# Exposed attention: one key tile of ten keeps its softmax weights whole, and its product with the values runs in fp32

## Chip, cores, metric

One core of one Trainium2 chip runs the kernel. The time is the device time of one execution in microseconds (us); the kernel before took 2972.27 us, the median of 3 runs (2970.56 to 2973.72).

## What is computed

A two-layer trunk over 1024 latent tokens and 256 context tokens, width 1024. Layer 0 mixes tokens with a convolution module, layer 1 with grouped-query attention (16 query heads of 64, 4 key/value heads); each layer ends in a SwiGLU FFN. The change touches the attention of layer 1 only:

```python
def gqa_sdpa(q, k, v):
    B, Q, H, Dh = q.shape
    qg = q.reshape(B, Q, N_KV_HEADS, KV_GROUP, Dh)
    s = jnp.einsum("bqkgd,bskd->bkgqs", qg, k).astype(jnp.float32) * (Dh ** -0.5)
    p = jax.nn.softmax(s, axis=-1).astype(v.dtype)
    o = jnp.einsum("bkgqs,bskd->bqkgd", p, v)
    return o.reshape(B, Q, H * Dh)
```

All 1280 keys (1024 latent, 256 context) take part for each latent query. Everything is fp32 in the reference.

## The kernel before

Matmuls run mostly in the type fp32r, which keeps fewer mantissa bits. So each operand is split into a high part (rounded to fp32r) and a low part (what is left), and a product is made of high x high, high x low and low x high. For softmax weights times values the kernel does less: the value tile holds high parts in its first 64 columns and low parts in the other 64 (`self.vst`, tile HR), so one matmul with the high part of the weights (L996) and one with the low part (L997) give all the products; the two halves are added at the end (L1007, L1008).

The attention works in **units**: one key/value head `t` (4) and one block of 128 queries `q` (8), with the 4 query heads of that group; 32 units in all. A first stream takes 16 units (blocks 0 to 3), a second one the other 16. A unit has two halves:

- `scores` (L959 to L983), for each of its 4 heads: q times k into 1280 columns of PSUM, as three chunks of 512, 512 and 256 columns with two matmuls each (L972); then VectorE scales, writes the row to SBUF and takes its minimum (L978), and ScalarE makes the exponential (L980).
- `values` (L985 to L1014), for each of ten key tiles `j` of 128 keys: four 128x128 transposes into one PSUM bank (L990), a ScalarE copy that rounds to the high part (L993), a VectorE subtraction that makes the low part (L994), and the two matmuls into the accumulator (L996, L997). After the tenth: the sums' reciprocal (L1001), a GpSimd copy that spreads it (L1003), two ScalarE copies and two VectorE additions that join the halves (L1007, L1008), two transposes (L1011), the final scaling (L1012) and the transfer to DRAM (L1279).

The generator `attn_stream` interleaves the `scores` of one unit with the `values` of the unit before. A list scheduler then sets the order on each engine by priority; the two value matmuls are pushed back by `self.lav` = 40 places. The first stream starts beside the rest of the q/k/v projections (`qr`, the background queue). When that queue is empty the stage is **exposed**: nothing but attention runs, and PSUM (8 banks of 512 fp32 columns) is shared out so: two score slots at columns 0 to 1279 and 1280 to 2559 (`sring = [0, TOK]`), which meet in bank 2 (columns 1024 to 1535), banks 5 and 6 for transposes, bank 7 for the accumulator. High and low parts go round in four slots (`ptring`, tile T2). The `values` of 15 of the first 16 units run in this exposed stage, from about 1655 to 1870 us. The second stream runs beside the output projection and the FFN and is not touched.

Short names below: **S512** and **S256** are score matmuls of 512 and 256 columns, **T** is one transpose, **AV** one value matmul. The S256 chunk of each slot lies in bank 2, which it shares with the other slot; it waits for the L978 that reads the other slot.

Of the kernel before, what the change touches and what calls it, by code (L numbers as in the profile page):

```python
# [8 lines left out]
F32 = mybir.dt.float32  # L9
# [45 lines left out]
class Kern:  # L55
# [928 lines left out]
    def values(self, t, Ps, sums, dst, done):  # L984
        nc, c = self.nc, self.c  # L985
        av = self.bank("av")
        for j in range(NJ):
            tp = self.bank("pt")
            for h in range(4):
                nc.tensor.transpose(tp[:, h * P:(h + 1) * P], Ps[h][:, j * P:(j + 1) * P], c["ident"])  # L990
            ph, pl = self.ptring[self.ptslot % len(self.ptring)]
            self.ptslot += 1
            nc.scalar.copy(ph, tp)  # L993
            nc.vector.tensor_tensor(pl, tp, ph.bitcast(F32), op=ALU.subtract)  # L994
            with self.later(self.lav):
                nc.tensor.matmul(av, lhsT=self.vst[:, t, j, :], rhs=ph, start=j == 0, stop=False)  # L996
                nc.tensor.matmul(av, lhsT=self.vst[:, t, j, :], rhs=pl, start=False, stop=j == NJ - 1)  # L997
            yield 0.87

        r = sums[:, 1, :]  # L1000
        nc.vector.reciprocal(r, sums[:, 0, :])  # L1001
        rx = self.sb(256)
        nc.gpsimd.tensor_copy(rx.rearrange("p (h d) -> p h d", d=HD), r.unsqueeze(2).to_broadcast([P, 4, HD]))  # L1003
        tmp = self.sb(256).rearrange("p (a q) -> p a q", q=P)
        v = av.rearrange("p (a b q) -> p a b q", b=2, q=P)
        for b, r, o in ((0, slice(0, 64), slice(64, 128)), (1, slice(64, 128), slice(0, 64))):
            nc.scalar.copy(tmp[r], v[o, :, b, :])  # L1007
            nc.vector.tensor_tensor(dst[r], v[r, :, b, :], tmp[r], op=ALU.add)  # L1008
        rb = self.bank("av")
        for a in range(2):  # L1010
            nc.tensor.transpose(rb[:, a * P:(a + 1) * P], rx[:, a * P:(a + 1) * P], c["ident"])  # L1011
        nc.vector.tensor_tensor(dst, dst, rb[:, 0:256].rearrange("p (a q) -> p a q", q=P), op=ALU.mult)  # L1012
        done()
        yield 0.1  # L1014
# [244 lines left out]
    def attention(self, final, qr):  # L1259
        nc, a, c = self.nc, self.a, self.c  # L1260
# [11 lines left out]
        def dst(q0):  # L1272
            def of(t, q):
                if (t, q % 4) == (NKV - 1, 3):
                    return self.olast, lambda: None
                st = self.sb(256).rearrange("p (a q) -> p a q", q=P)

                def done():
                    nc.gpsimd.dma_start(self.od[:, 2 * t:2 * t + 2, q * P:(q + 1) * P], st)  # L1279
                return st, done  # L1280
            return of
# [5 lines left out]
        self.sring = [TOK]  # L1287
        self.pring = [pr1[:, 0], prh[:, 0], pr1[:, 1], prh[:, 1], pr1[:, 2], prh[:, 2], prh[:, 3]]
        self.rate = 0.8
        self.lav = 40  # L1290
        self.bgq.append(qr)
        pr4 = None
        for us in self.attn_stream(units, (self.kub, kbuf), dst(0), True):
            if self.bgq:
                self.pump(self.rate * us)
            elif pr4 is None:
                pr4 = self.T("T5", [P, 3, TOK])
                self.pring = self.pring[:4] + [pr4[:, 0], pr4[:, 1], pr4[:, 2]] + self.pring[4:]
                self.set_banks(**alone)
                self.sring = [0, TOK]  # L1300
        self.lav = 40

        self.lo_dve = 1.0
        self.set_banks(mm=[6], st=[6], pt=[5], av=[7])
# [168 lines left out]
```

## Time and profile before

| what | value |
|---|---|
| median of 3 runs | 2972.27 us (2970.56 to 2973.72) |
| profiled execution, its own time | 2968.5 us |
| its span | 2966.6 us |
| TensorE (PE) busy | 2883.0 us, 97% |
| VectorE (DVE) busy | 1928.0 us, 65% |
| ScalarE (ACT) busy | 1197.4 us, 40% |
| GpSimd (POOL) busy | 240.6 us, 8% |
| exposed attention, two units | 29.40 us |

The profiled execution lies 3.8 us below the median of the three runs. The shares are means over the whole span. Matmul durations in the trace overlap, since matmuls are pipelined and their ends are modelled: what a matmul costs PE is the distance from its start to the next start. A transpose that follows another kind, or is followed by one, has its neighbour's start recorded some 0.1 us early.

### The profile page before, as it was taken

The numbers are of one execution on the slowest core, as the hardware profiler recorded it, in microseconds if no ns is written. First come the engines' busy times: TensorE is split into PE (matmuls) and PEld (weight loads), VectorE is DVE, ScalarE is ACT, GpSimd is POOL, SyncE is SP. The second block draws the span as 40 slices with busy tenths as digits, with TensorE's granted clock in tenths as the row PEclk, the third lists the DMA queues.
The fourth block names the chain that finished last, engine by engine and source line by source line (L and its number), as shares of the span: only waits on it lengthen the run. The fifth ranks groups of instructions, "written<-read, shape, count | busy, mean of one in ns | idle before, by whom it ended". The sixth has DMA issues, their size and how long they took to land.

```text
span 2966.6 us, 38934 instructions
## 1 busy us (share of the span) xinstructions
PE 2883.0 (97%) x14914; PEld 2399.0 (81%) x14914; DVE 1928.0 (65%) x3397; ACT 1197.4 (40%) x1966; POOL 240.6 (8%) x387
## 2 busy tenths in 40 slices
PE   8999989999999999999999999989999999999997
PEld 6888877888888888888877777767777778888886
DVE  6887887857555367333587899786666657543335
ACT  5222265532222135222344788645555543332222
POOL 0000001011112010000013111100100000000000
PEclk9999999999999999999999999989999999999999
DMA  6443434334355234333444211322212143442332
GB/s 246 134 123 97 122 129 168 116 115 136 127 167 174 65 124 156 97 96 96 134 163 161 61 49 45 107 79 79 84 56 84 62 136 108 146 142 93 95 97 64
DMA packets 132138, 336.35 MB, mean 113 GB/s; under 512 B 31472, under 2 KB 53008, under 8 KB 130800
## 3 DMA queue, kind: packets, MB, share of 16 engines
q1 hardware_dynamic: 78624, 222.59, 23.4%
q0 software_dynamic: 29408, 103.83, 10.7%
q10 hardware_dynamic: 23920, 7.44, 1.1%
q8 instruction: 117, 1.92, 0.3%
q14 instruction: 69, 0.57, 0.1%
HBM read 289.50 MB, written 38.93 MB: 111 GB/s over the span
## 4 chain that ended last, share of the span: by engine, by line
PE 87%; DVE 7%; issue 3%; DMA 1%; ACT 1%; POOL 0%; ACTq 0%; SPq 0%; DVEq 0%; POOLq 0%
PE ps L170 20%; PE ps L171 20%; PE ps L172 20%; PE ps L972 4%; PE ps L990 4%; PE ps L996 2%; PE ps L997 2%; PE ps L440 2%; PE ps L441 2%; PE ps L442 2%; PE ps L518 1%; PE ps L651 1%; PE ps L181 1%; PE ps L182 1%; PE ps L183 1%
## 5 line engine op out<-in xcount | busy, mean ns | idle before, releaser
L172 PE MATMUL ps<-T,wl 128*128 128x512 f32 (+1 forms) x2032 | 764.4, 376 | 4.8 <-DVE wl L146 4.8
L170 PE MATMUL ps<-T,wh 128*128 128x512 f32 (+1 forms) x2032 | 767.1, 378 | 0.5 <-DVE sm L794 0.4
L171 PE MATMUL ps<-T,wh 128*128 128x512 f32 (+1 forms) x1984 | 745.4, 376 | 0.0
L142 ACT CAST wh<-wr 128x1024 fp32r<-128x1024 f32 x285 | 299.3, 1050 | 747.5 <-PE ps L171 549.0
L146 DVE TENSOR_TENSOR wl<-wr,wh 128x1024 fp32r<-128x1024 f32 x279 | 341.2, 1223 | 284.3 <-ACT wh L142 279.5
L172 PEld LDWEIGHTS ps<-T,wl 128*128 128x128 f32 x2032 | 384.1, 189 | 74.8 <-DVE wl L146 5.2
L170 PEld LDWEIGHTS ps<-T,wh 128*128 128x128 f32 x2032 | 384.3, 189 | 69.7 <-ACT T L1333 1.7
L171 PEld LDWEIGHTS ps<-T,wh 128*128 128x128 f32 x1984 | 375.1, 189 | 67.2 <-DVE T L162 1.3
L171 PE MATMUL ps<-HS,wh 128*128 128x512 f32 (+1 forms) x768 | 297.4, 387 | 0.0
L994 DVE TENSOR_TENSOR T<-ps,T 128x512 fp32r<-128x512 f32 x320 | 216.9, 687 | 112.0 <-ACT T L993 111.2
L170 PE MATMUL ps<-HS,wh 128*128 128x512 f32 (+1 forms) x720 | 277.8, 388 | 0.0
L172 PE MATMUL ps<-HS,wl 128*128 128x512 f32 (+1 forms) x720 | 277.8, 386 | 0.0
L993 ACT CAST T<-ps 128x512 fp32r<-128x512 f32 x320 | 186.0, 586 | 195.0 <-PE ps L990 181.6
L990 PE MATMUL ps<-cst,T 128*128 128x128 f32 x1100 | 190.3, 275 | 4.6 <-DVE T L994 4.6
L978 DVE TENSOR_SCALAR_CACHE_REDUCE T<-ps,rq 128x1280 f32<-128x1280 f32 x110 | 170.0, 1546 | 27.4 <-PE ps L972 21.7
L825 DVE TENSOR_TENSOR T<-ps,T 128x512 f32<-128x512 f32 (+1 forms) x168 | 110.4, 663 | 115.5 <-PE ps L172 115.0
L990 PEld LDWEIGHTS ps<-cst,T 128*128 128x128 f32 x1100 | 133.4, 141 | 51.5 <-DVE T L994 32.5
L800 DVE TENSOR_TENSOR sm<-sm,ps 128x256 f32<-128x256 f32 (+1 forms) x88 | 54.6, 620 | 181.3 <-PE ps L172 181.2
L980 ACT ACTIVATE T<-T,mn 128x1280 f32<-128x1280 f32 x110 | 150.3, 1366 | 40.8 <-DVE T L978 40.3
L171 PEld LDWEIGHTS ps<-HS,wh 128*128 128x128 f32 x768 | 144.5, 188 | 27.4 <-DVE HS L162 0.2
L172 PEld LDWEIGHTS ps<-HS,wl 128*128 128x128 f32 x720 | 135.3, 188 | 26.8
L170 PEld LDWEIGHTS ps<-HS,wh 128*128 128x128 f32 x720 | 135.0, 188 | 26.1 <-ACT HS L159 0.8
(274 smaller groups left out, 4672.6 us busy)
## 6 DMA issues: line engine op xcount, KB each, us to landing
wr<-in_w SPq DMA_DIRECT2D x220, 512.0 KB, 3.5
q<-in_w SPq DMA_DIRECT2D x44, 512.0 KB, 3.4
wr<-in_pw SPq DMA_DIRECT2D x35, 512.0 KB, 3.6
HR<-in_wmodT POOLq DMA_DIRECT2D x56, 256.0 KB, 3.8
q<-in_wmodT POOLq DMA_DIRECT2D x56, 256.0 KB, 3.9
q<-qsd POOLq DMA_DIRECT2D x32, 256.0 KB, 3.2
wr<-in_wo SPq DMA_DIRECT2D x16, 512.0 KB, 3.4
qsd<-T POOLq DMA_DIRECT2D x14, 512.0 KB, 3.7
```

The lines of the kernel that those rows point to most:

```text
L142: nc.scalar.copy(hi, raw)
L146: nc.vector.tensor_tensor(lo, raw, hi.bitcast(F32), op=ALU.subtract)
L170: nc.tensor.matmul(out[:, :n], lhsT=wh, rhs=xh, start=k == 0, stop=False)
L171: nc.tensor.matmul(out[:, :n], lhsT=wh, rhs=xl, start=False, stop=False)
L172: nc.tensor.matmul(out[:, :n], lhsT=wl, rhs=xh, start=False, stop=k == nk - 1)
L825: nc.vector.tensor_tensor(yd, out[:, :c1 - c0], yd, op=ALU.add)
L972: nc.tensor.matmul(sc[:, k0:k0 + w], lhsT=q[:, h, :], rhs=kt[:, p * TOK + k0:p * TOK + k0 + w], start=p == 0, stop=p == 1)
L978: nc.vector.tensor_scalar(out=pt, in0=sc, scalar1=rq[:, h:h + 1], scalar2=None, op0=ALU.mult, op1=ALU.min, accum_out=mn)
L980: nc.scalar.activation(pt, pt, AF.Exp, bias=mn, scale=-1.0, accum_out=sums[:, 0, h:h + 1])
L990: nc.tensor.transpose(tp[:, h * P:(h + 1) * P], Ps[h][:, j * P:(j + 1) * P], c["ident"])
L993: nc.scalar.copy(ph, tp)
L994: nc.vector.tensor_tensor(pl, tp, ph.bitcast(F32), op=ALU.subtract)
```

## The change

In the exposed stage `self.whole` is `(5,)`, elsewhere it is empty. For key tile `j = 5` of each unit in that stage, the transposed weights are copied by ScalarE to a scratch tile `sm` in fp32, not rounded; the VectorE subtraction is left out; and one fp32 matmul, with the value tile read as fp32, takes the place of the two fp32r ones. The amount that the generator yields for this tile is 1.28, not 0.87; it would pace background work, and in this stage there is none.

```diff
@@ values
                 nc.tensor.transpose(tp[:, h * P:(h + 1) * P], Ps[h][:, j * P:(j + 1) * P], c["ident"])
+            if j in self.whole:
+                w = self.sm(512)
+                nc.scalar.copy(w, tp)
+                with self.later(self.lav):
+                    nc.tensor.matmul(av, lhsT=self.vst[:, t, j, :].bitcast(F32), rhs=w, start=False, stop=False)
+                yield 1.28
+                continue
             ph, pl = self.ptring[self.ptslot % len(self.ptring)]
@@ attention
         self.rate = 0.8
+        self.whole = ()
         self.lav = 40
@@ attention, where the background queue is empty
                 self.sring = [0, TOK]
+                self.whole = (5,)
         self.lav = 40
+        self.whole = ()
```

In the changed program the new matmul is L995 and stands 15 times; the lines after it are 7 higher (L994 becomes L1001, L996 and L997 become L1003 and L1004, L1001 becomes L1008, L1008 becomes L1015, L1011 becomes L1018, L1012 becomes L1019). The scheduler also orders the stage anew.

VectorE, around the end of one unit of the exposed stage. `T_12403` is the ring of high and low parts, `T_12401` and `T_12900` are weight buffers, `sb` the unit's result. Before:

```order
L978 TENSOR_SCALAR T_12401,mn<-ps,rq_9315 128x1280
L994 TENSOR_TENSOR T_12403<-ps,T_12403 128x512
L1008 TENSOR_TENSOR sb<-ps,sb 64x256
L994 TENSOR_TENSOR T_12403<-ps,T_12403 128x512
L978 TENSOR_SCALAR T_12900,mn<-ps,rq_9315 128x1280
L1008 TENSOR_TENSOR sb<-ps,sb 64x256
L994 TENSOR_TENSOR T_12403<-ps,T_12403 128x512
L1012 TENSOR_TENSOR sb<-sb,ps 128x256
L994 TENSOR_TENSOR T_12403<-ps,T_12403 128x512
L978 TENSOR_SCALAR T_12900,mn<-ps,rq_9315 128x1280
```

and with the change, at the same place:

```order
L978 TENSOR_SCALAR T_12401,mn<-ps,rq_9315 128x1280
L1001 TENSOR_TENSOR T_12403<-ps,T_12403 128x512 x2
L1015 TENSOR_TENSOR sb<-ps,sb 64x256
L1008 RECIPROCAL sums<-sums 128x4
L978 TENSOR_SCALAR T_12900,mn<-ps,rq_9315 128x1280
L1015 TENSOR_TENSOR sb<-ps,sb 64x256
L1001 TENSOR_TENSOR T_12403<-ps,T_12403 128x512
L1019 TENSOR_TENSOR sb<-sb,ps 128x256
L1001 TENSOR_TENSOR T_12403<-ps,T_12403 128x512
L978 TENSOR_SCALAR T_12900,mn<-ps,rq_9315 128x1280
```

The reciprocal has moved ahead of the L978 in the middle; two subtractions and one addition still stand before that L978.

TensorE, at the same place: from one slot's score matmuls to the transposes that end the unit. Before:

```order
L972 MATMUL ps<-T_12400,q 128x512 x4
L972 MATMUL ps<-T_12400,q 128x256 x2
L972 MATMUL ps<-T_12400,q 128x512 x2
L990 MATMUL ps<-cst,T_12401 128x128
L990 MATMUL ps<-cst,T_12900 128x128 x3
L972 MATMUL ps<-T_12400,q 128x512 x2
L990 MATMUL ps<-cst,T_12401 128x128
L990 MATMUL ps<-cst,T_12900 128x128 x3
L972 MATMUL ps<-T_12400,q 128x256 x2
L972 MATMUL ps<-T_12400,q 128x512
L1011 MATMUL ps<-cst,sb 128x128 x2
```

and with the change:

```order
L972 MATMUL ps<-KB,q 128x256 x2
L972 MATMUL ps<-KB,q 128x512 x2
L990 MATMUL ps<-cst,T_12401 128x128
L990 MATMUL ps<-cst,T_12900 128x128 x3
L972 MATMUL ps<-KB,q 128x512 x2
L990 MATMUL ps<-cst,T_12401 128x128
L990 MATMUL ps<-cst,T_12900 128x128 x3
L972 MATMUL ps<-KB,q 128x512 x4
L972 MATMUL ps<-KB,q 128x256 x2
L972 MATMUL ps<-KB,q 128x512
L1018 MATMUL ps<-cst,sb 128x128 x2
```

Before, the last S256 pair belongs to slot 1, and between the end of slot 0's six matmuls and it stand S512 x2, four T, S512 x2 and four T. With the change it belongs to slot 0, and between the last S512 of slot 1 and it stand four T and S512 x4.

## Rows read from the trace of the kernel before

**Rows 1.** The page: span, busy time of PE and DVE, and the shares of the chain that ended last by engine.

```profile
span 2966.6 us, 38934 instructions
...
PE 2883.0 (97%) x14914; PEld 2399.0 (81%) x14914; DVE 1928.0 (65%) x3397; ACT 1197.4 (40%) x1966; POOL 240.6 (8%) x387
...
PE 87%; DVE 7%; issue 3%; DMA 1%; ACT 1%; POOL 0%; ACTq 0%; SPq 0%; DVEq 0%; POOLq 0%
```

**Rows 2.** Busy time of each engine in stretches of two units of the exposed stage: stretch and its length, PE, PEld (weight loads), DVE, ACT, POOL, then granted TensorE clock, DMA share, GB/s.

```profile
1687.09:1716.51 29.42, 28.63 (x173) 23.54 (x173) 26.76 (x44) 23.83 (x41) 3.42 (x5) 1.00 0.09 28
1716.51:1745.91 29.40, 28.62 (x173) 23.48 (x173) 26.84 (x45) 23.94 (x41) 4.84 (x8) 1.00 0.29 73
1745.91:1775.31 29.40, 28.64 (x172) 23.49 (x172) 26.85 (x45) 23.82 (x41) 3.83 (x6) 1.00 0.09 28
1775.31:1804.74 29.43, 28.64 (x172) 23.50 (x172) 26.87 (x45) 23.93 (x41) 4.84 (x8) 1.00 0.29 72
1804.74:1834.15 29.41, 28.61 (x173) 23.48 (x173) 26.87 (x45) 23.93 (x41) 3.83 (x6) 1.00 0.09 28
```

**Rows 3.** PE in order of time at the end of a unit and after it: start, duration, instruction, count, and in brackets the idle time before it with what ended it.

```profile
1803.02 0.70 PE L972 MATMUL ps<-T,q 128*128 128x512 f32 x2
1803.57 0.60 PE L990 MATMUL ps<-cst,T 128*128 128x128 f32 x4
1804.74 0.73 PE L972 MATMUL ps<-T,q 128*128 128x256 f32 x3 [0.58 <-DVE HS L978]
...
1807.16 0.39 PE L997 MATMUL ps<-T,HR 128*128 128x512 f32 x1
...
1808.32 0.40 PE L996 MATMUL ps<-T,HR 128*128 128x512 f32 x1
1808.56 0.60 PE L990 MATMUL ps<-cst,T 128*128 128x128 f32 x4
```

**Rows 4.** The same at the end of the next unit.

```profile
1814.27 1.46 PE L972 MATMUL ps<-T,q 128*128 128x512 f32 x6
1815.58 0.27 PE L990 MATMUL ps<-cst,HS 128*128 128x128 f32 x1
...
1815.90 0.27 PE L990 MATMUL ps<-cst,T 128*128 128x128 f32 x1
1815.93 0.94 PE L972 MATMUL ps<-T,q 128*128 128x512 f32 x3
1816.71 0.27 PE L990 MATMUL ps<-cst,HS 128*128 128x128 f32 x1
...
1817.76 0.74 PE L972 MATMUL ps<-T,q 128*128 128x256 f32 x3 [0.21 <-DVE T L978]
```

**Rows 5.** DVE in order of time at the end of a unit (the unit of Rows 3).

```profile
1800.13 1.55 DVE L978 TENSOR_SCALAR_CACHE_REDUCE T<-ps,rq 128x1280 f32<-128x1280 f32 x1
1801.61 0.08 DVE L978 DVE_READ_ACCUMULATOR T<-ps,rq 128x1 f32 x1
1801.61 0.69 DVE L994 TENSOR_TENSOR T<-ps,T 128x512 fp32r<-128x512 f32 x1
1802.21 0.41 DVE L1008 TENSOR_TENSOR sb<-ps,sb 64x256 f32<-64x256 f32 x1
1802.55 0.67 DVE L994 TENSOR_TENSOR T<-ps,T 128x512 fp32r<-128x512 f32 x1
1803.14 1.54 DVE L978 TENSOR_SCALAR_CACHE_REDUCE HS<-ps,rq 128x1280 f32<-128x1280 f32 x1
...
1808.79 0.17 DVE L1001 RECIPROCAL sums<-sums 128x4 f32<-128x4 f32 x1
```

**Rows 6.** All engines in order of time shortly after the stage, two places where L978 has nothing to wait for but the last score matmul.

```profile
1875.25 0.39 PE L972 MATMUL ps<-KB,q 128*128 128x256 f32 x2
...
1875.68 1.55 DVE L978 TENSOR_SCALAR_CACHE_REDUCE T<-ps,rq 128x1280 f32<-128x1280 f32 x1 [0.29 <-PE ps L972]
...
1877.41 0.86 PE L972 MATMUL ps<-KB,q 128*128 128x256 f32 x4
```

**Rows 7.** PE in order of time in the convolution module's output product for the context, the longest stretch of fp32 matmuls in the program (L651, 256 columns); 64 matmuls of the program are 128 records of the trace.

```profile
404.08 7.07 PE L651 MATMUL ps<-T,wr 128*128 128x256 f32 x32
410.99 3.62 PE L651 MATMUL ps<-T,q 128*128 128x256 f32 x16
```

**Rows 8.** ACT in order of time: two roundings in a row, and, outside the stage, one copy of the same shape from PSUM that stays fp32 (L1333).

```profile
1811.26 1.27 ACT L993 CAST T<-ps 128x512 fp32r<-128x512 f32 x2 [0.80 <-PE ps L990]
1883.47 0.56 ACT L1333 COPY T<-ps 128x512 f32<-128x512 f32 x1
```

**Rows 9.** Who waited for whom from 1655 to 1862 us: total us, times, longest. Only rows that the change's queues touch.

```profile
POOL q L958 <- PE ps L972: 86.0, 13, 10.5
POOL od L1279 <- DVE sb L1012: 60.8, 7, 9.5
...
PEld ps L990 <- DVE T L994: 8.0, 35, 0.7
```

**Rows 10.** PE in order of time in the last unit, whose `values` have no scores beside them: the waits longer than the rest.

```profile
1861.16 0.66 PE L990 MATMUL ps<-cst,T 128*128 128x128 f32 x4 [0.26 <-DVE T L994]
1862.34 0.65 PE L990 MATMUL ps<-cst,T 128*128 128x128 f32 x4 [0.22 <-DVE T L994]
1867.52 0.66 PE L990 MATMUL ps<-cst,T 128*128 128x128 f32 x4 [0.38 <-DVE T L994]
1870.50 0.50 PE L996 MATMUL ps<-T,HR 128*128 128x512 f32 x1 [1.19 <-ACT T L993]
```

## The prediction

> **What bounds the kernel now.** I read the page first: PE is busy 97% of the span and holds 87% of the chain that ended last [rows 1], so in most places a microsecond of PE work is a microsecond of time. Then the stretches of the exposed stage: two units take 29.40 to 29.43 us, so 14.70 us each, with PE busy for 28.6 of 29.4, DVE for 26.8 and ACT for 23.9, at full clock [rows 2]. PE has the least slack, DVE little more. A busy PE is not all work, so I took the order in time. It shows PE waiting at the end of each unit, at the same instruction each time: the S256 pair that shares bank 2 with the other slot, and what ends the wait is L978 on DVE [rows 3, 4]. The stage is thus bound by PE plus one wait for DVE per unit, and the change moves both, in opposite directions.
>
> What PE's steps cost, from start to start. AV: 1807.16 to 1808.56 is six, 0.233 each [rows 3]. A T: 1815.58 to 1815.90 is three, 0.11 each [rows 4]. An S512 has the same 512 columns as an AV, so 0.233, and an S256 half, 0.115.
>
> What the waits cost. In rows 3 four T from 1803.57 end at 1804.01, and PE goes on at 1804.74: 0.73. In rows 4 four T from 1816.71 and one S512 end at 1817.38, and PE goes on at 1817.76: 0.38. There the six score matmuls from 1814.27 to 1815.58 take 1.31 where four S512 and two S256 need 1.16: a hidden wait of 0.15, again before an S256 pair. Together 1.26 in two units, **0.63 per unit**, so 14.07 of the 14.70 is work or waits too small to see.
>
> Why PE waits there: DVE is late. L978 (1.48 to the next instruction) ends at 1801.61, then come L994 (0.60), L1008 (0.34) and L994 (0.60), and the next L978 starts at 1803.14 only; PE goes on 1.60 after that start [rows 3, 5]. The scores it reads were complete long before.
>
> **The change part by part.**
>
> *PE: one fp32 matmul for two AV.* The trace of before has no fp32 matmul of 512 columns. The nearest row is L651, fp32 with 256 columns: 32 records from 404.08 to 410.99 are 0.216 each, two records per matmul [rows 7]. Time per record goes with columns, so 512 columns take 2 x 0.432 = 0.864. Two AV took 0.466. PE work grows by **0.40 per unit**, and 15 units have it: 6.0 us. Bounds: no less than two AV (0.466, growth 0), since it streams the same columns in two records; no more than four AV (0.93, growth 0.47), if each of its two records cost two. I take 0.40, by the row that does the same arithmetic.
>
> The Trainium skill, "FP8 and Floating Point Precision", section "TensorE Precision Notes", speaks against this change: it says that true FP32 makes four passes through the array. By that rule, at the AV price per pass, the growth would be the upper bound, 0.47, and the sum below 1 us more; the L651 rows show two records, each as long as two passes less the fixed part.
>
> *DVE: one L994 less.* It frees 0.60 per unit [rows 5], 9.0 us over 15 units. None of this is time by itself; it can only shorten the wait of 0.63.
>
> *ACT: a copy for a rounding.* L993 takes 0.59 alone and 1.27 for two [rows 8]; an fp32 copy of the same shape from PSUM took 0.56 [rows 8]. I take 0; ACT has 5.5 us free in two units [rows 2] that would cover a few hundredths.
>
> *Buffers and queues.* The copy goes to a ring of three scratch tiles that nothing else uses in this stage, so each has three units' time to come free: 0. The ring of high and low parts serves nine tiles, not ten. On GpSimd's queue the load of the next q (L958) now stands behind the unit's transfer to DRAM (L1279) and the spreading copy; it waited for the score matmuls anyway, for 86 us in all, as L1279 waits for L1012 [rows 9]. The q it loads is needed a unit later, 14.7 us, so I cost this at nothing; without that cover it would be the length of a transfer once per unit.
>
> *The new order and the wait.* I walked one unit of the changed order by hand with these prices: L978 to PE 1.60, L994 0.60, L1008 0.34, the last score matmul's slot to L978 0.20 (S256 pair from 1875.25 ends at 1875.48, L978 starts at 1875.68 [rows 6]). Of the unit's four L978, two are ready 0.7 us or more before PE needs them and one is ready just in time, with 0.01 to spare. The fourth is the one in the middle of the listed orders. PE has four T and four S512 between the last score matmul that it reads and the S256 pair that waits for it: 0.44 + 0.93 = 1.37. The chain needs 0.20 + 1.60 = 1.80. So PE waits **0.43**, however free DVE is. Nor is DVE free much sooner. From the start of the L978 before, DVE needs 1.48 and then two L994, one L1008 and a reciprocal (0.17 [rows 5]), 3.19 in all; PE needs 1.60, four S512, two S256 halves and four T, then 0.20, which is 3.40. The limit passes from DVE's queue to PE's own order, and of the 0.60 that DVE frees only 0.63 - 0.43 = 0.20 comes back.
>
> *The last unit* has no scores to hide behind; its transposes wait for L994 and its AV for ACT, 0.2 to 1.2 us at a time [rows 10]. One L994 less helps there, by its 0.60 at most and by nothing if ACT ends the wait: I take 0.5 once.
>
> **Sum.** 15 x (0.40 - 0.20) = +3.0, less 0.5: **+2.5 us**. The profiled execution took 2968.5, so it would be 2971.0. The median of the three runs, 2972.27, lies 3.8 above that execution, so for a median I add the 2.5 there: **2974.8 us**.
>
> **The rivals.**
>
> *A second wait (slower).* The L978 with 0.01 us to spare gates the S256 pair that opens slot 1. PE has three T, AV, T, AV, four T and two AV before it, 8 x 0.11 + 4 x 0.233 = 1.81, against the chain's 1.80. From L978 to PE it is 1.60 in rows 3 and 1.73 in rows 6 (1875.68 to 1877.41). If 1.73 holds here, PE waits 0.12 at this place and 0.56 at the other: 0.25 more per unit, +3.7, so +6.2 and 2978.5. It decides from 1.61 on. For it: rows 6. Against: in the stage itself the distance is 1.60 (1803.14 to 1804.74).
>
> *The wait goes away (no loss, or a small gain).* If PE reached both places after L978, a unit would be 14.07 + 0.40 = 14.47, 0.23 less than now: -3.5 with the 15 units, -4 with the last: 2968.3. For it: DVE's load falls from 13.4 to 12.8 per unit while PE's rises. Against: 1.80 against 1.37 is a matter of PE's own order.
>
> *fp32 costs no more than the pair.* Then 15 x (0 - 0.20) - 0.5 = -3.5 and the same 2968.8. Against: L651 [rows 7].
>
> *The change does nothing*, because the exposed stage is not limited by these steps: 2972.3. Against: PE's chain share [rows 1] and the waits on L978.
>
> **How the numbers follow.** Below, "same" means within 0.2%, 5.9 us, about what a measurement of this kernel can tell from no change. The forecast, a loss between 1 and 5 us, gets 0.58. The second wait gets 0.18, split about evenly over that bound since its price may be smaller. The wait that goes away and the cheap fp32 matmul get 0.15 together, mostly inside the bound, since even with no wait left the gain is 3.5 to 4. No effect gets 0.05, and 0.04 is left for the ends of the stage. Of these, 0.03 of the 0.15 and half of the last make faster 0.05; half of the second wait and half of the last make slower 0.11; same has 0.84. The range: at the low end most of the case without a wait, 2969.5; at the high end the second wait with 1.73 and a little of four passes (15 x 0.07 = 1.0), 2979.5.
>
> **What would show it.** L995 as two records some 0.43 apart, 30 in all. Two units in 29.6 to 30.0 us, PE busy up, DVE down by some 1.2 in two units. The wait before an S256 pair once per unit, still ended by L978, and that L978 itself ended by PE's matmuls or back to back behind L994, near 0.4 us. If two units take less than 29.2, or the waits on L978 are gone, the middle step is wrong; if L995 takes less than 0.8, the price is; if the two units are above 30.2, the second wait came.

## The result and the profile after

The changed kernel takes 2977.22 us, the median of 16 runs (2972.5 to 2979.47); the kernel before, run beside it, takes 2971.92 (2967.64 to 2975.49, 16 runs). The ratio is 1.0017, with a 95% interval of 1.001 to 1.0024: 5.1 us longer, between 3.0 and 7.1. The forecast was +2.5, inside 0.2%; the result, 0.17%, lies inside 0.2% too, though its interval reaches 0.24%, and is a small loss.

The page of after: span, busy time, and the shares of the chain that ended last by engine [rows 1]. Its own time is 2978.86.

```profile
span 2976.9 us, 38897 instructions
...
PE 2892.9 (97%) x14914; PEld 2401.9 (81%) x14914; DVE 1918.9 (64%) x3382; ACT 1195.5 (40%) x1966; POOL 239.9 (8%) x387
...
PE 88%; DVE 7%; issue 3%; DMA 2%; ACT 1%; ACTq 0%; POOL 0%; SPq 0%; DVEq 0%; POOLq 0%
```

The two profiled executions differ by 10.4 us, the medians by 5. The stage tells how much of it is the change. ScalarE's table load ahead of the first exponential starts at 1587.81 before and at 1591.69 after; the first copy behind the stage starts at 1883.47 and at 1891.76. From the one to the other it is 295.66 and 300.07: the stage costs **4.4 us more**. The other 6 lie in code that is the same in both, 3.9 of them ahead of the stage.

Two units after, the stretches placed as in [rows 2]: stretch and length, busy time of PE, PEld, DVE, ACT and POOL, granted clock, DMA share, GB/s.

```profile
1780.55:1810.57 30.02, 29.45 (x173) 23.29 (x174) 25.61 (x43) 23.86 (x41) 4.83 (x8) 1.00 0.27 69
1795.56:1825.58 30.02, 29.44 (x173) 23.33 (x174) 25.63 (x43) 23.84 (x41) 4.88 (x8) 1.00 0.28 71
```

A unit is 15.01 us, 0.31 more than 14.70. PE is busy 0.8 more in two units, DVE 1.2 less.

PE of after in order of time: the fp32 matmul, then the end of a unit [rows 3, 4].

```profile
1786.21 1.02 PE L995 MATMUL ps<-sm,HR 128*128 128x512 f32 x2
1787.06 1.04 PE L990 MATMUL ps<-cst,T 128*128 128x128 f32 x8
...
1791.62 0.39 PE L1004 MATMUL ps<-T,HR 128*128 128x512 f32 x1
1791.86 0.97 PE L972 MATMUL ps<-KB,q 128*128 128x256 f32 x4
1792.67 0.27 PE L990 MATMUL ps<-cst,HS 128*128 128x128 f32 x1
...
1793.02 0.71 PE L972 MATMUL ps<-KB,q 128*128 128x512 f32 x2
1793.58 0.27 PE L990 MATMUL ps<-cst,HS 128*128 128x128 f32 x1
...
1793.93 1.18 PE L972 MATMUL ps<-KB,q 128*128 128x512 f32 x4
1795.39 0.73 PE L972 MATMUL ps<-KB,q 128*128 128x256 f32 x3 [0.28 <-DVE T L978]
```

The L995 pair costs 0.85 from start to start. At the unit's end, four T from 1793.58 end at 1794.02 and four S512 at 1794.95, and PE goes on at 1795.39: a wait of 0.44. At 1791.86 four score matmuls, two of 256 and two of 512 columns, take 0.81 where they need 0.70: a hidden wait of 0.11. So a unit is 14.07 of work as before, 0.385 for the dearer matmul (0.85 less 0.466), and 0.44 and 0.11 of waits: 15.005.

The hidden 0.11 is a weight load. PE's own row shows no gap: the AV before it starts at 1791.62 and takes 0.233, so PE was free at 1791.85. But the weights of the first S256 were not loaded ahead. PEld stood idle for 0.28 until L978 released the load at 1791.86, 1.62 behind L978's start at 1790.24 and together with the matmul, and the second S256 starts 0.22 behind the first, not 0.115:

```profile
1791.86 0.53 PEld L972 LDWEIGHTS ps<-KB,q 128*128 128x128 f32 x4 [0.28 <-DVE T L978]
```

```profile
1792.08 0.51 PE L972 MATMUL ps<-KB,q 128*128 128x256 f32 x2
```

It is so at each such place. In eight units of after, all 16 S256 pairs whose weight load waited for L978 have 0.22 to 0.23 between their two matmuls; in eight units of before, 12 such pairs have the same and the 17 whose load ran ahead have 0.11 to 0.12.

DVE of after at the same place [rows 5].

```profile
1790.24 1.55 DVE L978 TENSOR_SCALAR_CACHE_REDUCE T<-ps,rq 128x1280 f32<-128x1280 f32 x1 [0.19 <-PE ps L972]
...
1791.72 1.28 DVE L1001 TENSOR_TENSOR T<-ps,T 128x512 fp32r<-128x512 f32 x2
1792.92 0.40 DVE L1015 TENSOR_TENSOR sb<-ps,sb 64x256 f32<-64x256 f32 x1
1793.25 0.16 DVE L1008 RECIPROCAL sums<-sums 128x4 f32<-128x4 f32 x1
1793.77 1.55 DVE L978 TENSOR_SCALAR_CACHE_REDUCE T<-ps,rq 128x1280 f32<-128x1280 f32 x1 [0.36 <-PE ps L972]
```

Before, L978 followed the instruction ahead of it without a gap; here DVE is idle for 0.36 ahead of it, and what ends that is PE's score matmul. From its start to PE it is 1.62 (1793.77 to 1795.39). The waits from 1655 to 1875 us say the same of the whole stage (total us, times, longest): L978 waited for PE 17 times where its result goes to the buffers T; the 7 waits of those that go to HS are 2.1 us more.

```profile
DVE T L978 <- PE ps L972: 5.2, 17, 0.4
PE ps L972 <- DVE T L978: 4.3, 14, 0.7
```

In the kernel before, the group of L978 from 1655 to 1880 us (busy time, mean ns of one, idle time before it and what ended most of it) has 0.6 us of waiting for PE in all:

```profile
L978 DVE TENSOR_SCALAR_CACHE_REDUCE T<-ps,rq 128x1280 f32<-128x1280 f32 x45 | 69.4, 1543 | 0.7 <-PE ps L972 0.6
```

The last unit of after [rows 10]: the waits of over 0.2 us from 1860 to 1882.

```profile
1870.30 0.66 PE L990 MATMUL ps<-cst,T 128*128 128x128 f32 x4 [1.41 <-DVE T L1001]
1871.48 0.66 PE L990 MATMUL ps<-cst,T 128*128 128x128 f32 x4 [0.22 <-DVE T L1001]
1878.98 0.97 PE L972 MATMUL ps<-KB,q 128*128 128x256 f32 x4 [0.62 <-DVE T L978]
```

### The profile page after: what moved, and what is told of

Its sections match the earlier page's. It is cut to its first block, busy times and chain, and to the rows that moved or that the text cites. A ratio compares the mean times of both kernels' runs of the same rounds, so it can differ in the third digit from the quotient of the medians.

```text
span 2976.9 us, 38897 instructions
## 1 busy us (share of the span) xinstructions
PE 2892.9 (97%) x14914; PEld 2401.9 (81%) x14914; DVE 1918.9 (64%) x3382; ACT 1195.5 (40%) x1966; POOL 239.9 (8%) x387
## 4 chain that ended last, share of the span: by engine, by line
PE 88%; DVE 7%; issue 3%; DMA 2%; ACT 1%; ACTq 0%; POOL 0%; SPq 0%; DVEq 0%; POOLq 0%
PE ps L170 20%; PE ps L172 20%; PE ps L171 20%; PE ps L972 5%; PE ps L990 4%; PE ps L1003 2%; PE ps L1004 2%; PE ps L440 2%; PE ps L441 2%; PE ps L442 2%; PE ps L518 1%; PE ps L651 1%; PE ps L181 1%; PE ps L182 1%; PE ps L183 1%
## 5 line engine op out<-in xcount | busy, mean ns | idle before, releaser
L170 PE MATMUL ps<-T,wh 128*128 128x512 f32 (+1 forms) x2032 | 767.9, 378 | 0.6 <-DVE sm L794 0.4
L170 PEld LDWEIGHTS ps<-T,wh 128*128 128x128 f32 x2032 | 384.5, 189 | 70.0 <-ACT T L1343 1.7
L1001 DVE TENSOR_TENSOR T<-ps,T 128x512 fp32r<-128x512 f32 x305 | 205.9, 687 | 118.3 <-ACT T L1000 116.1
L170 PE MATMUL ps<-HS,wh 128*128 128x512 f32 (+1 forms) x720 | 277.8, 388 | 0.0
L1000 ACT CAST T<-ps 128x512 fp32r<-128x512 f32 x305 | 174.3, 586 | 200.4 <-PE ps L990 188.1
L978 DVE TENSOR_SCALAR_CACHE_REDUCE T<-ps,rq 128x1280 f32<-128x1280 f32 x110 | 170.2, 1547 | 33.7 <-PE ps L972 27.0
L170 PEld LDWEIGHTS ps<-HS,wh 128*128 128x128 f32 x720 | 135.0, 188 | 26.2 <-ACT HS L159 0.8
```

The lines of the kernel that those rows point to most:

```text
L170: nc.tensor.matmul(out[:, :n], lhsT=wh, rhs=xh, start=k == 0, stop=False)
L978: nc.vector.tensor_scalar(out=pt, in0=sc, scalar1=rq[:, h:h + 1], scalar2=None, op0=ALU.mult, op1=ALU.min, accum_out=mn)
```

## Experiments

Two theories stood against each other. **A**: where PE waits at the unit's end is set by PE's own order, 1.80 us of hand-off (0.20 from the last score matmul to L978, 1.60 from there to PE) against the work that PE has in between. **B**: VectorE's load sets it, and less work there brings the wait down. In n_before and n_after A, widened to all hand-offs of the unit, is called theory C; a_lav36 and b_lav36 go by the same walk through the order.

The table holds what was measured in the stage. A unit is the eighth part of the distance between the starts of the multiplication that ends a unit (L1012 of before) and of the one eight units on, at granted clock 1.00 (2.4 GHz). Work is 14.07, with 0.385 for each fp32 matmul in place of a pair and 0.233 less for an AV left out. The waits are the difference. One weight load of 0.11 per unit, that of the pair at the unit's end, is held back in before as in after and so counts as work. The two-unit stretches above gave 15.01 for after.

| kernel | from, to (us) | unit | work | waits |
|---|---|---|---|---|
| before | 1701.15, 1818.80 | 14.71 | 14.07 | 0.64 |
| after | 1691.51, 1811.44 | 14.99 | 14.455 | 0.54 |
| e_relief | 1704.00, 1820.01 | 14.50 | 14.07 | 0.43 |
| e_price | 1692.45, 1815.18 | 15.34 | 14.455 | 0.89 |
| e_one | 1701.62, 1817.45 | 14.48 | 13.84 | 0.64 |
| a_last | 1691.04, 1810.21 | 14.90 | 14.455 | 0.44 |
| a_lav30 | 1705.15, 1825.38 | 15.03 | 14.455 | 0.57 |
| a_lav36 | 1691.43, 1811.75 | 15.04 | 14.455 | 0.59 |
| a_lav60 | 1693.93, 1819.25 | 15.67 | 14.455 | 1.21 |
| e_two | 1705.55, 1830.63 | 15.64 | 14.84 | 0.80 |
| n_before | 1701.80, 1820.60 | 14.85 | 14.07 | 0.78 |
| n_after | 1703.05, 1824.28 | 15.15 | 14.455 | 0.70 |

Single times stand beside a median of 2970.92 of the kernel before for a_lav36, b_lav36, n_before and n_after, and beside one run of it, 2976.44, for the rest; since runs of the kernel before alone spread over 8 us, their verdicts rest on the unit, not on the time. Each edit is to the changed kernel unless it says before.

**e_relief**: two fp32r matmuls with the whole weights rounded, no subtraction.

```diff
-                w = self.sm(512)
+                w = self.sm(512, F32R)
...
-                    nc.tensor.matmul(av, lhsT=self.vst[:, t, j, :].bitcast(F32), rhs=w, start=False, stop=False)
+                    nc.tensor.matmul(av, lhsT=self.vst[:, t, j, :], rhs=w, start=False, stop=False)
+                    nc.tensor.matmul(av, lhsT=self.vst[:, t, j, :], rhs=w, start=False, stop=False)
```

> The changed kernel without its fp32 matmul: key tile 5 of the exposed units has no subtraction, but still two fp32r value matmuls, both with the high part (the low part of that tile's weights is left out). PE work as before, DVE 0.60 us less per unit. Theory A (the wait is set by PE's own order: 1.80 us from the last score matmul that L978 reads to the S256 pair that waits, less the PE work between them): the order has 1.37 us between them at the end of the unit and 2.27 at the other place, so one wait of 0.43 and none else: 14.07 + 0.43 = 14.50 us per unit, 29.0 for two. Rival B (DVE's load sets the wait): all of the 0.60 comes back, 14.10 per unit, 28.2 for two. Rival C (the fp32 matmul disturbs its neighbours): as A.

Measured: 14.50 per unit, 2970.74. With the price gone and the subtraction still left out, a unit is 0.2 under the kernel before and a wait of 0.43 stays. This is the 0.20 that the prediction gave to the subtraction, seen without the price, in an order of its own, and as A has it.

**e_price**: the subtraction put back, its result unread.

```diff
                 nc.scalar.copy(w, tp)
+                nc.vector.tensor_tensor(self.dead, tp, w, op=ALU.subtract)
...
                 self.whole = (5,)
+                self.dead = self.acc(512)
```

> The changed kernel with the subtraction kept: key tile 5 of the exposed units has its fp32 matmul, and VectorE still makes a low part, which nobody reads. PE work 0.39 us more per unit than before, DVE as before. Theory A: PE 14.07 + 0.39 = 14.46, and waits between the changed kernel's 0.55 (order) and the 0.63 of before (DVE's queue): 15.0 to 15.1 per unit, 30.0 to 30.2 for two; the freed subtraction is thus worth at most 0.1. Rival B: the whole 0.60 of DVE is lost again, 15.01 + 0.60 = 15.6 per unit, 31.2 for two.

Measured: 15.34 per unit, between the two; 2982.37. Both missed. Beside the fp32 matmul, the subtraction is worth 0.33 to 0.35 per unit, more than the 0.20 of the prediction. In DVE's rows L978 stands back to back again, behind a join and two subtractions (L1002 here):

```profile
1780.32 0.41 DVE L1016 TENSOR_TENSOR sb<-ps,sb 64x256 f32<-64x256 f32 x1
1780.65 1.27 DVE L1002 TENSOR_TENSOR T<-ps,T 128x512 fp32r<-128x512 f32 x2
1781.85 1.53 DVE L978 TENSOR_SCALAR_CACHE_REDUCE HS<-ps,rq 128x1280 f32<-128x1280 f32 x1
```

**e_one**: one fp32r matmul with the rounded weights; the low part of tile 5 is left out.

```diff
-                w = self.sm(512)
+                w = self.sm(512, F32R)
...
-                    nc.tensor.matmul(av, lhsT=self.vst[:, t, j, :].bitcast(F32), rhs=w, start=False, stop=False)
+                    nc.tensor.matmul(av, lhsT=self.vst[:, t, j, :], rhs=w, start=False, stop=False)
```

> Key tile 5 of the exposed units with one fp32r value matmul and no subtraction (the low part of that tile's weights is left out). PE 0.233 less than before, DVE 0.60 less. Theory A: 14.07 - 0.23 = 13.84, and the order has 1.81, 2.51 and 2.97 us of PE work where L978 needs 1.80, so a wait of 0.0 to 0.1: 13.9 per unit, 27.8 for two. Rival B: 14.70 - 0.60 = 14.1 per unit, 28.2 for two, with waits on L978 left.

Measured: 14.48, 2968.01: 0.6 and 0.4 above what was expected. One AV less than in e_relief, and the unit is the same. PE and DVE of e_one at a unit's end:

```profile
1786.10 0.27 PE L990 MATMUL ps<-cst,HS 128*128 128x128 f32 x1
...
1786.45 0.47 PE L972 MATMUL ps<-KB,q 128*128 128x512 f32 x1
1787.43 0.73 PE L972 MATMUL ps<-KB,q 128*128 128x256 f32 x3 [0.50 <-DVE T L978]
```

```profile
1784.01 0.69 DVE L1001 TENSOR_TENSOR T<-ps,T 128x512 fp32r<-128x512 f32 x1
1784.89 0.42 DVE L1015 TENSOR_TENSOR sb<-ps,sb 64x256 f32<-64x256 f32 x1 [0.20 <-issue]
1785.23 0.67 DVE L1001 TENSOR_TENSOR T<-ps,T 128x512 fp32r<-128x512 f32 x1
1785.83 1.53 DVE L978 TENSOR_SCALAR_CACHE_REDUCE T<-ps,rq 128x1280 f32<-128x1280 f32 x1
```

Four T and one S512 end at 1786.77 and PE goes on at 1787.43: 0.66. The order had enough work for PE by A; L978 stands behind DVE's queue instead. A does not hold for every order.

**a_last**: slot 1's S256 pair is issued behind its four S512 in the exposed stage.

```diff
...
+            if self.lastk:
+                ch.sort(key=lambda c: -c[1])
+            for k0, w in ch:
...
                 self.sring = [0, TOK]
+                self.lastk = True
```

> The changed kernel, with one thing more: in the exposed stage slot 1's S256 pair is issued after its four S512, not before them. Theory A (the second wait is real and stands before that pair): the wait of 0.11 at slot 1 goes, since only slot 0's pair still waits for the other slot; the wait of 0.44 stays (1.37 us of PE work before it, as now): 15.01 - 0.11 = 14.90 per unit, 29.8 for two. Rival C (the 0.11 that the unit is above my sum comes from the fp32 matmul's neighbours, not from this wait): 15.01, 30.0 for two.

Measured: 14.90, 0.11 less than 15.01; 2975.68. The hidden wait at slot 1 was there, and this is its size. The weights of slot 1's pair are now loaded ahead (load at 1792.00, matmul at 1792.23), and its two matmuls are 0.12 apart.

**a_lav30**, **a_lav60**, **a_lav36**: value matmuls pushed back by another number of places in the exposed stage.

```diff
                 self.sring = [0, TOK]
+                self.lav = 30
                 self.whole = (5,)
```

> The changed kernel with the value matmuls pushed back by 30 places instead of 40 in the exposed stage, so that TensorE has at least 1.81 us of work of its own between the last score matmul that any L978 reads and the S256 pair that waits for it (the changed kernel has 1.37 at the unit's end and 1.81 elsewhere). Theory A, the wait at the unit's end is set by TensorE's own order (1.80 needed, 1.37 there): the wait of 0.44 goes and a unit falls from 15.01 us to 14.5 to 14.7, the kernel by 5 to 8 us. Theory B, VectorE's queue at the unit's end sets it as well (as in the run with one value matmul for tile 5): a wait of 0.4 or more stays and a unit is 14.9 to 15.1.

> The same with 60 places: by the order TensorE has 2.07, 1.84 and 1.81 us of work between score matmuls and the S256 pairs that wait. Theory A: a unit in 14.5 to 14.7 us, as with 30. Theory B: 14.9 to 15.1, with a wait at the unit's end that VectorE's queue sets.

> The changed kernel with 36 places, to see what the fp32 tile does beside that order. If the price alone counted: 0.385 us per unit above the run before this one, 14.84 if that has 14.45. The walk gives 14.99, since the order made around the fp32 matmul has more waits: 14.95 to 15.05.

Measured: 15.03 with 30 (2976.67), 15.67 with 60 (2988.62), 15.04 with 36 (2979.12). A's expectation of 14.5 to 14.7 fell twice. With 30 the unit is in B's range: at its end L978 starts at 1807.73 behind a join and two subtractions without a gap, and PE waits 0.38 (1808.95 to 1809.33). With 60 the unit is longer than B expected too. With 36 it lies in the range of the walk. PE and DVE of a_lav60 at a unit's end:

```profile
1800.78 0.27 PE L990 MATMUL ps<-cst,HS 128*128 128x128 f32 x1
...
1801.55 0.27 PE L990 MATMUL ps<-cst,T 128*128 128x128 f32 x1
1802.54 0.51 PE L972 MATMUL ps<-KB,q 128*128 128x256 f32 x2 [0.72 <-DVE T L978]
```

```profile
1797.90 1.55 DVE L978 TENSOR_SCALAR_CACHE_REDUCE T<-ps,rq 128x1280 f32<-128x1280 f32 x1 [0.54 <-PE ps L972]
...
1799.41 0.42 DVE L1015 TENSOR_TENSOR sb<-ps,sb 64x256 f32<-64x256 f32 x1
1799.75 1.27 DVE L1001 TENSOR_TENSOR T<-ps,T 128x512 fp32r<-128x512 f32 x2
1800.95 1.53 DVE L978 TENSOR_SCALAR_CACHE_REDUCE T<-ps,rq 128x1280 f32<-128x1280 f32 x1
```

Eight T from 1800.78 end at 1801.66 and PE goes on at 1802.54: 0.88. One L978 waited for PE (0.54), and the next came 3.05 behind it with a join and two subtractions between. The two hand-offs are in series: a late score matmul delays the first L978, and the first delays the second.

**e_two**: tiles 3 and 6 in place of tile 5.

```diff
-                self.whole = (5,)
+                self.whole = (3, 6)
```

> Two key tiles of ten (3 and 6) with whole weights and an fp32 matmul, in place of tile 5 alone. The order then has 3.15, 1.81 and 1.81 us at the places that wait. Theory A, each fp32 matmul costs 0.385 us more than its pair and the wait goes with the order: 14.07 + 0.77 = 14.84, with a hidden wait of 0.1 up to 15.0 us per unit. Theory B, the wait of 0.44 at the unit's end stays whatever the order: 15.3 to 15.4 us per unit.

Measured: 15.64, above both; 2984.66. The wait on L978 did go from the unit's end. Another came, PE and ACT of e_two:

```profile
1811.95 0.60 PE L990 MATMUL ps<-cst,T 128*128 128x128 f32 x4
1812.30 1.17 PE L972 MATMUL ps<-T,q 128*128 128x512 f32 x4
1813.85 0.66 PE L990 MATMUL ps<-cst,T 128*128 128x128 f32 x4 [0.38 <-ACT sm L993]
```

```profile
1810.86 1.36 ACT L980 ACTIVATE HS<-HS,mn 128x1280 f32<-128x1280 f32 x1
...
1812.34 0.36 ACT L1014 COPY sb<-ps 64x256 f32<-64x256 f32 x1
1812.72 0.59 ACT L1000 CAST T<-ps 128x512 fp32r<-128x512 f32 x1
1813.21 0.59 ACT L993 COPY sm<-ps 128x512 f32<-128x512 f32 x1
```

The four T wait for a transpose bank that ScalarE's copy empties; the copy stands behind an exponential, a copy for the join and a rounding. Four T and four S512 end at 1813.32: 0.53 lost.

**n_before**, **n_after**: the subtractions of the exposed stage on 128 of 512 columns, in the kernel before and in the changed one.

```diff
-            nc.vector.tensor_tensor(pl, tp, ph.bitcast(F32), op=ALU.subtract)
+            n = self.subn; nc.vector.tensor_tensor(pl[:, :n], tp[:, :n], ph.bitcast(F32)[:, :n], op=ALU.subtract)
...
-                self.sring = [0, TOK]
+                self.sring = [0, TOK]; self.subn = 128
```

> The kernel before with the subtraction that makes the low parts done on 128 of 512 columns in the exposed stage (the rest of each low part is left out), so that VectorE has some 3.5 us less to do per unit. The scheduler orders the stage anew. Theory C, a unit is one cycle of hand-offs from TensorE to L978 (or ScalarE's copy) and back, in the order that TensorE has, and VectorE's load does not set it: walking the listed order with the durations of the traces, where the waits at the unit's end are behind only 1.37 us of TensorE's own work, gives 14.70 us per unit, as before; 14.6 to 14.8. Theory B, VectorE's queue makes the waits: they go, and a unit is 14.1 to 14.2 us.

> The same in the changed kernel, some 3.2 us less for VectorE per unit. Theory C: the walk gives 15.02 us per unit, as now (15.01); 14.9 to 15.1. Theory B: 14.46 to 14.6.

Measured: 14.85 and 15.15, each a little over C's range and 0.6 above B's; 2975.67 and 2982.86. DVE was busy 79.7 us in eight units where the kernel before has 107.4, and the unit is 0.14 *longer*. PE and DVE of n_before at a unit's end:

```profile
1773.24 0.60 PE L990 MATMUL ps<-cst,T 128*128 128x128 f32 x4
1773.59 1.17 PE L972 MATMUL ps<-KB,q 128*128 128x512 f32 x4
1775.05 0.75 PE L972 MATMUL ps<-KB,q 128*128 128x256 f32 x3 [0.29 <-DVE T L978]
```

```profile
1772.37 0.42 DVE L1008 TENSOR_TENSOR sb<-ps,sb 64x256 f32<-64x256 f32 x1 [0.16 <-ACT sb L1007]
1773.44 1.55 DVE L978 TENSOR_SCALAR_CACHE_REDUCE T<-ps,rq 128x1280 f32<-128x1280 f32 x1 [0.65 <-PE ps L972]
```

The scheduler made the order of after here too: four T and four S512 behind the last score matmul, 1.37. They end at 1774.61 and PE goes on at 1775.05: 0.44, with DVE idle for 0.65 ahead of L978. This is A's 0.43 in another kernel, and theory B falls for these two orders; in those of e_one, e_price and a_lav60 L978 does stand behind DVE's queue. Of n_before's 0.78 of waits another 0.11 is a held weight load (the pair from 1786.37 is 0.22 apart); where the last 0.2 goes stays open. The order changed with the load, so the two were not varied singly.

**b_lav36**: the kernel before with 36 places.

> The kernel before with the value matmuls pushed back by 36 places instead of 40 in the exposed stage, nothing else. The same walk gives 14.45 us per unit against 14.69 for the kernel before: 0.24 less per unit and some 3.8 us over the stage, a time 3 to 4.5 us under the kernel before. Rival: as with 30 and 60 places in the changed kernel, the waits come back elsewhere and a unit is 14.7 or more, a time no lower than before.

Measured: 2971.06, the median of 12 runs, beside 2970.92 of 15; ratio 0.9998, interval 0.9989 to 1.0007 (3.3 us less to 2.1 more), without the one of the 12 that took 3425.64. The expected gain of 3 to 4.5 is not seen; 3.8 lies just outside the interval, 3.0 inside it. Its profile, of that one run, has a mean granted clock of 0.75 in the stage (1.00 in the others), so no unit can be read from it, and where the gain went stays open.

**b_lav60**: the kernel before with 60 places.

> The kernel before with the value matmuls pushed back by 60 places instead of 40 in the exposed stage; TensorE has 2.97, 2.51 and 1.81 us of work at the places that wait. Theory A, what the change gave back of the wait (0.63 to 0.55 with the second one) came from the order that the scheduler makes and not from the subtraction left out: with this order a unit falls from 14.70 to between 14.1 and 14.4 us, without fp32. Theory B, VectorE's ten subtractions per unit keep its queue late whatever the order: a unit in 14.6 to 14.8 us.

Measured: 14729.75, and nothing follows from it. All of PE was slow in that run, in code far from the edit: the matmuls of L170 are recorded with a mean of 1421 ns, those of after with 378.

No version here that keeps all parts of the sum is shown to be faster than the kernel before: e_relief and e_one, the only ones in the table with a shorter unit, leave out the low part of tile 5.

## Why the prediction was right, and where it was off

**The fp32 matmul: right.** 0.864 was forecast from a 256-column row [rows 7]; the pair takes 0.85 and the growth is 0.385, not 0.40. As two records 0.43 apart, 30 in all:

```profile
L995 PE MATMUL ps<-sm,HR x30: 590/592/593, 1666.2 to 1875.7; 128*128 128x512 f32 x30
```

By the four passes of the Trainium skill ("FP8 and Floating Point Precision", section "TensorE Precision Notes") an estimate at the AV price is 0.93. The trace shows 0.85, which is 3.65 AV; whether there are fewer than four passes or one costs less than an AV, no run here tells. The "fixed part" by which the prediction made two passes out of 0.216 is in no row either: two S256 cost 0.23, as much as one S512.

**The wait at the unit's end: right, in place, cause and size.** Forecast 0.43 from 1.80 against 1.37, ended by an L978 that itself waits for PE; measured 0.44, with DVE idle 0.36 ahead of L978. It came again at 0.43 in e_relief and at 0.44 in n_before. The bound did pass from DVE's queue to PE's order.

**The L978 with 0.01 to spare: wrong.** This is the step of the sum that failed. The prediction let it cost nothing and gave a second wait a chance of 0.18 at 0.25 per unit in all. 0.11 is lost there; a_last shows it by taking it away. It is 0.11 x 15 = 1.6 us. The hundredth by which the hand-off grew, from 1.60 to 1.62, does not explain it. What the prediction left out is that the S256's weight load waits for L978 as the matmul does: the release came in time for the matmul and 0.11 late for its load. The rival's 1.73 [rows 6] was this and no slower hand-off. There too the load starts 1.61 behind L978 (1875.68 to 1877.29), and the matmul 0.12 later, while PE is still busy with another, so that nothing is lost and the pair is 0.12 apart:

```profile
1877.29 1.01 PEld L972 LDWEIGHTS ps<-KB,q 128*128 128x128 f32 x6 [0.16 <-DVE T L978]
```

```profile
1877.53 0.51 PE L972 MATMUL ps<-KB,q 128*128 128x256 f32 x2
```

The rival thus came with its own price of 0.12 at this place. The other half of its 0.25, at the unit's end, was not new: there the pair is 0.22 apart before the change too (from 1804.74 and from 1817.76), so that 0.11 is in the 14.07, and of the hidden 0.15 in [rows 4] 0.11 is the same (the pair from 1814.77). So the waits fell from 0.63 to 0.55, and what came back is 0.08 per unit, not 0.20.

**The last unit: not seen.** 0.5 less was forecast. Before, its four waits are 2.05 us [rows 10]; after, the three are 2.25, and the longest, 1.41, is a transpose that waits for a subtraction. The order of this unit changed as well.

**ACT, buffers, GpSimd's queue: right at nothing.** ACT is busy 23.9 in two units as before, and from 1655 to 1875 us no wait of PE is ended by a DMA.

**The sum.** 15 x (0.385 - 0.08) = 4.6, and nothing for the last unit: 4.6, against 4.4 in the stage of the two traces and 5.1 (3.0 to 7.1) in the runs. The forecast of 2.5 lies just under that interval: 0.5 too low for the last unit, 1.6 for the second wait and 0.1 for 0.44 in place of 0.43, with the matmul 0.2 too high. The time, 2977.22, lies inside the range of 2969.5 to 2979.5, whose high end was set with the second wait in it; the case thought likeliest, a loss of 1 to 5 us, holds the 4.4 of the stage and just misses the 5.1 of the runs. Two units took 30.02, between the 30.0 of the forecast and the 30.2 that was to mark the second wait: that mark was set too high, since it counted the wait at 0.25.

**What the explanation can't do.** A's rule gives the wait once the order is known and L978 is not held up by DVE's own queue. It did not tell what another order would cost: of the expectations worked out by it, those of e_relief, a_last and a_lav36 came, n_before and n_after missed by 0.05, e_price, e_one, a_lav30 and a_lav60 fell, b_lav36's gain was not seen, and e_two lost its time at ScalarE instead. In all twelve orders of the table between 0.43 and 1.21 us per unit went into waits, whatever was taken off an engine. That every order of this stage must wait is not shown.

## What to carry to other kernels

When work is taken off an engine that releases the bounding one, count the bounding engine's own work between what it hands over and what it waits for: the length of the hand-off less that work is the wait that stays, however free the other engine becomes. A place with a slack of a hundredth of a microsecond should be costed as a wait, not as nothing: a matmul that is released just in time still lacks its weights, which cost 0.11 here. And where a list scheduler sets the order, less work on one engine gives another order, so that a saving must be read from that order, not from the load: here a quarter less work on VectorE made a unit longer.

## Not expected of the hardware

An fp32 matmul scales with columns as simply as two slow records: 0.216 each for 256 columns [rows 7], 0.43 for 512. ScalarE's fp32 copy from PSUM takes as long as its rounding, 0.59 each in the rows of e_two. On VectorE the subtraction of 128 columns was recorded with a mean of 288 ns, that of 512 with 686, so a quarter of the columns is 0.42 of the time.
